# Stick-breaking attention with queries on partitions: weights from sigmoids and a backward product scan, in place of softplus sums on TensorE

## The chip, the cores and the metric

The kernel runs on one core of a Trainium2 chip. Its engines are TensorE (PE; its weight loads are listed apart as PEld), VectorE (DVE), ScalarE (ACT), GpSimd (POOL) and SyncE (SP). The metric is the device time of one execution in microseconds.

## The reference

Two transformer blocks are applied one after the other to x, 512 tokens of 1024 features, in float32. The change touches one stage of the second block, the stick-breaking attention with 16 heads of 64 features:

```
z = einsum("bhqd,bhkd->bhqk", q, k) / sqrt(64)
mask = key_pos < q_pos
log_beta = log_sigmoid(z)
log_1m = where(mask, log_sigmoid(-z), 0)
suffix = cumsum(log_1m, axis=keys, reverse=True) - log_1m
wts = where(mask, exp(log_beta + suffix), 0)
out = einsum("bhqk,bhkd->bhqd", wts, v)
```

The weight of key j for query i is thus sigmoid(z_ij) times the product of sigmoid(-z_il) over the keys l between j and i. The stage has a projection to q, k and v before it and an output projection with a residual after it.

## The kernel before

Activations lie with features on partitions and the 512 tokens along the free side, in eight tiles of 128 features. Products keep float32's precision by splitting each operand into two parts (hi and lo) of the type fp32r: ScalarE casts hi, VectorE subtracts to get lo, and a product is three passes (lo by hi, hi by lo, hi by hi; `mm3`, lines 171 to 176). One block of weights (128 output columns) is loaded by SyncE's queue (`raw`), split (`whi` on ScalarE, line 101; `wlo` on VectorE, line 102) and used in 24 products of 512 columns (`gemm`). `Feed` hands the blocks out in a fixed order, loaded three and split two blocks ahead, into buffers of a ring.

Heads are worked on in eight pairs k, since two heads of 64 features fill 128 partitions; half 0 and half 1 of a pair are the two heads. The scores of a head are held with keys on partitions: block j of 128 keys against the queries that can see it, 512, 384, 256 and 128 columns, in three PSUM banks (`ZG`: keys 0; keys 1 and 3; keys 2). Per half-step:

- `scores` (line 1108): twelve products from the parts of q and k (line 1117), then for each of three groups the softplus max(z, 0) + ln(1 + exp(-|z|)) in three ScalarE passes (1121 to 1123) and one VectorE pass (1124), a causal select on GpSimd (1094), and a split into parts `sp`.
- `sums` (line 1129): twenty products that add -softplus, summed over the later keys, onto the scores in PSUM, with a triangle or ones (`ntri`) as the other operand (1134).
- `weights` (line 1137): exp of the result, the causal select again, and a split into parts `w`.
- `values` (line 1147): twelve products with v (line 1154), and a split of the output (`Oh`, `Ol`).

TensorE's order in this stage is the order of the code (`manual_schedule`); the other engines' lists are ordered by the scheduler. Between the steps of a pair the code puts the projections for the next pairs (q and k by `proj`, v in two halves, then turned to tokens on partitions by four transposes in `vparts`), and for the last two pairs parts of the output projection (`out_part`).

Of the kernel before, what the change touches and what calls it, by code (L numbers as in the profile page):

```python
# [25 lines left out]
# columns of the packed per-feature vectors  # L26
# [9 lines left out]
# square constants  # L36
# [3 lines left out]
# order of the 128-column blocks of w_in  # L40
# [13 lines left out]
def block_kernel(ctx: ExitStack, tc: tile.TileContext, xT, pT, cols, cst, wA, wBr, wO, w13, w2, wPG, wPL,  # L54
# [107 lines left out]
    feed.add([bQKV[8], bQKV[9], bQKV[0], bQKV[10], bQKV[11]])  # L162
    for k in range(KD - 1):
        if k == KD - 2:
            feed.mark((2, 0, 0, 1))
        feed.add(([bQKV[9 + 2 * (k + 2)]] if k < KD - 2 else [bO[0]]) + [bQKV[k + 1]] + ([bQKV[8 + 2 * (k + 2)]] if k < KD - 2 else []))
    feed.add([bO[m] for m in range(1, KD)])
# [59 lines left out]
    def rowbc(pool, tag, c4, name):  # L227
        """[128, 4] per token -> psum [128, 512], the same on every partition."""
# [12 lines left out]
    def norm_rows(pool, tag, ss, name, rc=None):  # L241
        """1/rms of each token, spread over the partitions."""
# [15 lines left out]
    # =========================== block 1, mixers ===========================  # L258
# [30 lines left out]
    with ExitStack() as ca:  # L289
# [73 lines left out]
        # (the slots of the residual are free until the output projection)  # L363
# [29 lines left out]
        # g4: per token and head, [beta, alpha, i, f]  # L393
# [6 lines left out]
        # softplus(alpha), softplus(-f)  # L400
# [24 lines left out]
        # gl: [-exp(a_log) softplus | log f], negated: lg2[:, 0] = -g, lg2[:, 1] = -log f  # L425
# [9 lines left out]
        # cum[:, 0] inclusive cumsums within a block, cum[:, 1] block totals; [.., 0] g, [.., 1] log f  # L435
# [3 lines left out]
        bge = GP.tile([P, NB, H], F32, name="bge")    # beta exp(gc)  # L439
# [5 lines left out]
        kds = GP.tile([P, NB, H], F32, name="kds")    # exp(gtot - gc)  # L445
# [116 lines left out]
        # rj[:, j]: exponent row for the keys of block j  # L562
# [117 lines left out]
        def solve(i):  # L680
            """U = (I + beta K K^T * decay)^-T of chunk i, and what follows from it"""
# [67 lines left out]
        def state(i):  # L749
# [24 lines left out]
            # head norm  # L774
# [6 lines left out]
            # q carries rq / sqrt(dk)  # L781
# [127 lines left out]
    # =========================== per-layer embedding gate, then the recurrent mixer ===========================  # L909
    RP = ctx.enter_context(tc.tile_pool(name="RP", bufs=1, side="right", reuse_waits="tile"))  # L910
    B = xset(RP, "B")
    with ExitStack() as cb:
# [29 lines left out]
        # R1: block 1's final norm; R2: block 2's first norm of its result  # L942
# [24 lines left out]
        ls2 = PB.tile([P, KD], F32, name="ls2")      # -2 log sigmoid(lam)  # L967
# [7 lines left out]
        def branch(n):  # L975
            """input blocks 2n and 2n + 1, convolved, with their parts"""
# [17 lines left out]
        def recur(n, xc, xp_):  # L994
            hi, lo = parts_of(load_raw(aRI[n]), 8, PB, "rw")
            y, ti, v, a = b2("y"), b2("ti"), b2("v"), b2("a")
            for m in range(2):
# [4 lines left out]
                V.tensor_scalar(y[:, m, :], y[:, m, :], 1.0, ls2[:, k:k + 1], op0=ALU.add, op1=ALU.mult)   # -log_a / 2  # L1002
# [6 lines left out]
            # 1 - a = v (1 + a), sqrt(1 - a^2) = sqrt(v) (1 + a)  # L1009
# [5 lines left out]
            hs = b2("hs")                                # half of the state  # L1015
# [4 lines left out]
        def outgate(k, h_):  # L1020
            """h gelu(gate), gelu(x) = x / 2 (1 + tanh(c (x + 0.044715 x^3)))"""
# [20 lines left out]
        # the first block's result, normed  # L1042
# [29 lines left out]
    # =========================== stick-breaking attention ===========================  # L1072
    with ExitStack() as cs:
        pmm = cs.enter_context(tc.tile_pool(name="pmm3", bufs=2, space=PSUM, reuse_waits="tile"))
        psz = cs.enter_context(tc.tile_pool(name="psz", bufs=2, space=PSUM, reuse_waits="tile"))
# [5 lines left out]
        ntri = SB.tile([P, 2, P], F32R, name="ntri")  # L1081
        S.activation(ntri[:, 0, :], CST[:, C_TL, :], AF.Copy, scale=-1.0)
        S.activation(ntri[:, 1, :], ones, AF.Copy, scale=-1.0)
# [3 lines left out]
        # blocks of keys in three banks: 0 | 1, 3 | 2  # L1087
# [3 lines left out]
        def causal(t, js):  # L1091
            for j in js:
                o = ZP[j][1]
                G.affine_select(t[:, o:o + P], t[:, o:o + P], pattern=[[1, P]], base=0, channel_multiplier=-1,
                                compare_op=ALU.is_gt, fill=0.0)
# [8 lines left out]
        def blk(ts, j):  # L1104
            g, o = ZP[j]
            return ts[g][:, o:o + NW[j]]

        def scores(half, qp, kp):
            p0 = 64 * half
            zs = [psz.tile([P, T], F32, tag=f"z{g}", bufs=2, name=f"z{g}") for g in range(2)] + [zlast[:, half, :]]  # L1110
            sps = []
            for g, (w, js) in enumerate(ZG):
                z = zs[g]
                for j in js:
                    ks = slice(j * P, (j + 1) * P)
                    for n, (a, b) in enumerate(((kp[1], qp[0]), (kp[0], qp[1]), (kp[0], qp[0]))):
                        TE.matmul(blk(zs, j), a[p0:p0 + 64, ks], b[p0:p0 + 64, j * P:], start=(n == 0 and j == js[0]),  # L1117
                                  stop=False, skip_group_check=True)
                e = SB.tile([P, T], F32, tag="e", bufs=4, name="e")
                es = e[:, 0:w]  # L1120
                S.activation(es, z[:, 0:w], AF.Abs)
                S.activation(es, es, AF.Exp, scale=-1.0)
                S.activation(es, es, AF.Ln, bias=onec)
                V.scalar_tensor_tensor(es, z[:, 0:w], 0.0, es, op0=ALU.max, op1=ALU.add)
                causal(e, js)
                sps.append(parts(f"sp{g}", es, w, 1))
            return zs, sps
# [9 lines left out]
        def weights(zs):  # L1137
            out = [None] * 3
            for g in (2, 1, 0):
                w, js = ZG[g]  # L1140
                e = SB.tile([P, T], F32, tag="e", bufs=4, name="e2")
                S.activation(e[:, 0:w], zs[g][:, 0:w], AF.Exp)
                causal(e, js)
                out[g] = parts(f"w{g}", e[:, 0:w], w, 1)
            return out

        def values(k, half, wts, vp):
            po = pn.tile([P, T], F32, tag="nr", name="po")
            n = 0
            for g in (2, 1, 0):  # L1150
# [10 lines left out]
        with tc.issue_after(last.ins):  # L1161
            S.preload_act_table_set("natural_log_exp_and_others")
        def evac(ps, w):
# [241 lines left out]
```

## Time and profile before

| | |
|---|---|
| three timed runs | 2107.92, 2108.28 (median), 2108.46 us |
| span of the profiled execution, first to last instruction | 2105.6 us |
| busy: TensorE, VectorE, ScalarE, GpSimd | 2074.4, 1087.7, 825.9, 241.7 us |
| attention stage, first scores to the last pair's values | 1457.1 to 1704.7 us |

The profile gives no time for the profiled execution apart from its span, which lies 2.7 us under the median. Busy times are sums of durations; where operations overlap (TensorE's above all), the distance between starts says what one costs.

### The profile page before, as it was taken

The numbers are of one execution on the slowest core, as the hardware profiler recorded it, in microseconds if no ns is written. First come the engines' busy times: TensorE is split into PE (matmuls) and PEld (weight loads), VectorE is DVE, ScalarE is ACT, GpSimd is POOL, SyncE is SP. The second block draws the span as 40 slices with busy tenths as digits, with TensorE's granted clock in tenths as the row PEclk, the third lists the DMA queues.
The fourth block names the chain that finished last, engine by engine and source line by source line (L and its number), as shares of the span: only waits on it lengthen the run. The fifth ranks groups of instructions, "written<-read, shape, count | busy, mean of one in ns | idle before, by whom it ended". The sixth has DMA issues, their size and how long they took to land.

```text
span 2105.6 us, 24834 instructions
## 1 busy us (share of the span) xinstructions
PE 2074.4 (99%) x9946; PEld 1726.6 (82%) x9946; DVE 1087.7 (52%) x1461; ACT 825.9 (39%) x1213; POOL 241.7 (11%) x293
## 2 busy tenths in 40 slices
PE   8999999999999999999999999999999999999998
PEld 7778899888888888877788888887888888888887
DVE  5667454555444432779954444334666554444322
ACT  4333232333233222546633233224778743233221
POOL 0111000131000000252310000001212220000011
PEclk9999999999999999999999999999999999999999
DMA  4211111333322333322223323332111122323332
GB/s 166 70 61 60 51 50 41 107 123 100 100 92 99 95 99 97 110 80 82 87 93 99 100 92 97 94 99 90 42 59 61 40 71 90 100 92 98 93 100 68
DMA packets 53667, 181.73 MB, mean 86 GB/s; under 512 B 5808, under 2 KB 7984, under 8 KB 53552
## 3 DMA queue, kind: packets, MB, share of 16 engines
q1 hardware_dynamic: 53408, 180.05, 27.0%
q8 instruction: 78, 1.28, 0.3%
q14 instruction: 37, 0.30, 0.0%
q10 hardware_dynamic: 144, 0.10, 0.0%
HBM read 178.03 MB, written 2.10 MB: 86 GB/s over the span
## 4 chain that ended last, share of the span: by engine, by line
PE 92%; DVE 4%; issue 1%; DMA 1%; ACT 1%; POOL 0%; SPq 0%; POOLq 0%; DVEq 0%
PE psmm L174 19%; PE psmm L175 19%; PE psmm L176 19%; PE psd L174 5%; PE psd L175 5%; PE psd L176 5%; PE z L1134 2%; PE po L1154 1%; PE z L1117 1%; PE pU L732 1%; PE pX L727 1%; DVE wlo L102 1%; DVE xc L988 1%; PE psv L174 1%; PE psv L176 1%
## 5 line engine op out<-in xcount | busy, mean ns | idle before, releaser
L101 ACT CAST whi<-raw 128x1024 fp32r<-128x1024 f32 (+1 forms) x333 | 344.2, 1035 | 923.2 <-issue 363.5
L102 DVE TENSOR_TENSOR wlo<-raw,whi 128x1024 fp32r<-128x1024 f32 (+1 forms) x333 | 411.3, 1236 | 292.9 <-ACT whi L101 292.7
L174 PE MATMUL psmm<-Bh,wlo 128*128 128x512 f32 x1032 | 402.4, 390 | 0.0
L175 PE MATMUL psmm<-Bl,whi 128*128 128x512 f32 x1032 | 402.0, 390 | 0.1
L176 PE MATMUL psmm<-Bh,whi 128*128 128x512 f32 x1032 | 401.9, 389 | 0.0
L174 PE MATMUL psmm<-Ah,wlo 128*128 128x512 f32 x832 | 332.9, 401 | 4.0 <-DVE wlo L102 3.1
L176 PE MATMUL psmm<-Ah,whi 128*128 128x512 f32 x832 | 325.2, 391 | 0.0
L175 PE MATMUL psmm<-Al,whi 128*128 128x512 f32 x832 | 324.4, 390 | 0.6 <-DVE Al L190 0.6
L174 PEld LDWEIGHTS psmm<-Bh,wlo 128*128 128x128 f32 x1032 | 193.7, 188 | 41.2 <-DVE wlo L102 0.2
L175 PEld LDWEIGHTS psmm<-Bl,whi 128*128 128x128 f32 x1032 | 193.8, 188 | 40.4 <-DVE Bl L190 0.5
L176 PEld LDWEIGHTS psmm<-Bh,whi 128*128 128x128 f32 x1032 | 193.8, 188 | 39.9
L217 POOL TENSOR_TENSOR ss<-ss,sq 128x512 f32<-128x512 f32 x55 | 84.9, 1550 | 1133.3 <-issue 803.9
L174 PE MATMUL psd<-Hh,wlo 128*128 128x512 f32 x506 | 196.8, 389 | 0.0
L175 PE MATMUL psd<-Hl,whi 128*128 128x512 f32 x506 | 196.8, 389 | 0.0
L176 PE MATMUL psd<-Hh,whi 128*128 128x512 f32 x506 | 196.8, 389 | 0.0
L174 PEld LDWEIGHTS psmm<-Ah,wlo 128*128 128x128 f32 x832 | 156.4, 188 | 37.2 <-DVE wlo L102 4.5
L176 PEld LDWEIGHTS psmm<-Ah,whi 128*128 128x128 f32 x832 | 156.2, 188 | 33.7
L175 PEld LDWEIGHTS psmm<-Al,whi 128*128 128x128 f32 x832 | 156.6, 188 | 30.3 <-DVE Al L190 1.1
L871 DVE TENSOR_TENSOR u<-psmm,R 128x512 f32<-128x512 f32 x66 | 45.6, 691 | 194.2 <-PE psmm L176 194.2
L867 DVE TENSOR_TENSOR s<-psmm,R 128x512 f32<-128x512 f32 x66 | 45.6, 692 | 137.0 <-PE psmm L176 134.1
L176 PEld LDWEIGHTS psd<-Hh,whi 128*128 128x128 f32 x506 | 95.0, 188 | 19.9
L174 PEld LDWEIGHTS psd<-Hh,wlo 128*128 128x128 f32 x506 | 95.0, 188 | 19.7
(500 smaller groups left out, 2617.6 us busy)
## 6 DMA issues: line engine op xcount, KB each, us to landing
raw<-in_f SPq DMA_DIRECT2D x120, 512.0 KB, 3.5
raw<-in_w SPq DMA_DIRECT2D x60, 512.0 KB, 3.5
raw<-in_wA SPq DMA_DIRECT2D x43, 512.0 KB, 3.5
raw<-in_bQKV SPq DMA_DIRECT2D x24, 512.0 KB, 3.5
raw<-in_aIn SPq DMA_DIRECT2D x16, 512.0 KB, 3.6
raw<-in_f SPq DMA_DIRECT2D x16, 384.0 KB, 3.0
x<-in_xT SPq DMA_DIRECT2D x16, 256.0 KB, 3.4
raw<-in_wBr SPq DMA_DIRECT2D x8, 512.0 KB, 3.5
```

Source lines behind the costliest of these rows:

```text
L101: copied[0] = S.copy(hi[:, :nk, :], raw[:, :nk, :])
L102: V.tensor_tensor(lo[:, :nk, :], raw[:, :nk, :], hi[:, :nk, :].bitcast(F32), op=ALU.subtract)
L174: TE.matmul(ps, l, xh, start=(first and i == 0), stop=False)
L175: TE.matmul(ps, h, xl, start=False, stop=False)
L176: TE.matmul(ps, h, xh, start=False, stop=(last and i == n - 1))
L217: eng.tensor_tensor(self.acc, self.acc, sq, op=ALU.add)
L727: heads(lambda h: TE.matmul(pX[:, h], Nm[:, h, :], odd(U)[:, h], start=True, stop=True))
L732: heads(lambda h: TE.matmul(pU[:, h], Tt[:, h, :], X[:, h], start=True, stop=True))
L867: V.tensor_tensor(s1, p1, R, op=ALU.mult)
L871: V.tensor_tensor(u, p3, R, op=ALU.mult)
L988: V.scalar_tensor_tensor(ac, cx[:, j:j + T], col("aconv", 4 * k + j), ac, op0=ALU.mult, op1=ALU.add)
L1134: TE.matmul(blk(zs, j)[:, (jj - j) * P:], ntri[:, 0 if jj == j else 1, :], sp[:, o:o + NW[jj]], start=False, stop=(jj == j and sp is sps[g ...
```

## The change

Scores are now held with queries on partitions: query block i against the keys it can see, 128 (i + 1) columns, again in three PSUM banks (`QB`: queries 3; queries 2 and 0; queries 1), now one buffer each instead of two. 1/rms of the query's token and 1/8 become the per-partition scale `rq` of the activation, so q is split straight from PSUM, without the scaling by R. Per group, ScalarE writes `om` = sigmoid(-z) and `be` = sigmoid(z); GpSimd sets the masked part of `om` to 1 and of `be` to 0; VectorE runs a scan backward over the keys, pr = max(om * state, anew), where `anew` is 1 at the last column of each query block and 0 elsewhere, so that the product starts anew there; and `be` is multiplied by `pr` moved by one column. `turn` transposes the ten 128x128 blocks of weights on TensorE into three banks, in the old layout, and splits them. The softplus, the sums, and their split are gone. In the loop over pairs, the scores of the next head are issued ahead of the transposes of the one before; K of the next pair is now projected in the pair before it instead of two pairs ahead, and a fourth block of the output projection is begun early.

```diff
-        zlast = psz.tile([P, 2, 256], F32, tag="z2", bufs=1, name="zlast")
-        R = norm_rows(pn, "nr", ss, "R6")
+        psz = cs.enter_context(tc.tile_pool(name="psz", bufs=1, space=PSUM, reuse_waits="tile"))
+        rc6 = norm_cols(pn, "nr", ss)
+        R = norm_rows(pn, "nr", ss, "R6", rc6)
+        rq = SB.tile([P, 2, NB], F32, name="rq")
+        for n, c in enumerate((0.125, -0.125)):
+            V.tensor_scalar(rq[:, n], rc6, c, None, op0=ALU.mult)
+        QB = ((0, 3, 0, 512), (1, 2, 0, 384), (1, 0, 384, 128), (2, 1, 0, 256))
+        ZW = ((0, 512), (512, 512), (1024, 256))
         def scores(half, qp, kp):
+            for g in range(3):
+                qbs = [(i, o, w) for g_, i, o, w in QB if g_ == g]
+                for i, o, w in qbs:
+                    qs = slice(p0, p0 + 64), slice(i * P, (i + 1) * P)
+                    for n, (a, b) in enumerate(((0, 1), (1, 0), (0, 0))):
+                        TE.matmul(zs[g][:, o:o + w], qp[a][qs], kp[b][p0:p0 + 64, 0:w], start=(n == 0 and o == 0),
+                                  stop=(n == 2), skip_group_check=True)
+                c0, cw = ZW[g]
+                for t, n in ((om, 1), (be, 0)):
+                    for i, o, w in qbs:
+                        S.activation(t[:, c0 + o:c0 + o + w], zs[g][:, o:o + w], AF.Sigmoid, scale=rq[:, n, i:i + 1])
+                    d0 = c0 + qbs[0][1] + qbs[0][2] - P
+                    d = t[:, d0:c0 + cw].rearrange("p (n c) -> p n c", c=P)
+                    G.affine_select(d, d, pattern=[[0, len(qbs)], [-1, P]], base=0, channel_multiplier=1,
+                                    compare_op=ALU.is_gt, fill=float(n))
+                sl = slice(c0, c0 + cw)
+                V.tensor_tensor_scan(pr[:, sl][:, ::-1], om[:, sl][:, ::-1], anew[:, sl][:, ::-1], 1.0,
+                                     op0=ALU.mult, op1=ALU.max)
+                V.tensor_tensor(be[:, c0:c0 + cw - 1], be[:, c0:c0 + cw - 1], pr[:, c0 + 1:c0 + cw], op=ALU.mult)
+            return be
+        def turn(be):
+            out = []
             for g, (w, js) in enumerate(ZG):
+                t = pn.tile([P, T], F32, tag="nr", name="t2") if g == 2 else psz.tile([P, T], F32, tag=f"t{g}", name=f"t{g}")
                 for j in js:
+                    for i in range(j, NB):
+                        c = next(ZW[g_][0] + o for g_, i_, o, _ in QB if i_ == i) + j * P
+                        o = ZP[j][1] + (i - j) * P
+                        TE.transpose(t[:, o:o + P], be[:, c:c + P], ident)
+                out.append(parts(f"w{g}", t[:, 0:w], w, 1))
-        def sums(zs, sps):
-            for j in (3, 2, 1, 0):
-                for jj in range(3, j - 1, -1):
-                    g, o = ZP[jj]
-                    for sp in (sps[g][1], sps[g][0]):
-                        TE.matmul(blk(zs, j)[:, (jj - j) * P:], ntri[:, 0 if jj == j else 1, :], sp[:, o:o + NW[jj]],
-                                  start=False, stop=(jj == j and sp is sps[g][0]), skip_group_check=True)
             for k in range(KD):
+                more = k < KD - 1
+                wb = scores(1, q, kk)
+                wt = turn(wa)
                 if more:
+                    kk, q = proj(k + 1, 1), qn
+                    values(k, 0, wt, v)
                     vhi, vlo = feed.next(bQKV[k + 1])
                     pv = pmm.tile([P, T], F32, tag="mm", name="psv")
                     mm3(pv, [(vhi[:, c, :], vlo[:, c, :], A[c]) for c in range(4)], last=False)
+                    wa = scores(0, q, kk)
+                    wt = turn(wb)
                     mm3(pv, [(vhi[:, c, :], vlo[:, c, :], A[c]) for c in range(4, 8)], first=False)
                     vt = evac(pv, 2)
+                    if k < KD - 2:
+                        qn = proj(k + 2, 0)
+                    else:
+                        out_part(0, range(0, 6))
+                    values(k, 1, wt, v)
+                    v = vparts(vt)
                 else:
+                    out_part(1, range(0, 7))
+                    values(k, 0, wt, v, psz, "z0")
+                    out_part(0, range(6, 7))
+                    wt = turn(wb)
+                    out_part(2, range(0, 7), psz, "z1")
+                    values(k, 1, wt, v, psz, "z0")
+            out_part(3, range(0, 7), psz, "z2")
+            for m in range(4):
                 out_part(m, range(7, 8))
```

On TensorE, where one pair's V transposes (`pv`) are followed by the next half-step, the list before goes on with the twenty sums into the score banks (`z`, `zlast`; `sp` are the parts of softplus), and then the other head's scores from q and k:

```order
L1175 MATMUL pv<-CST,qk 128x128 x4
L1134 MATMUL z_11500<-sp1l,ntri 128x128
L1134 MATMUL z_11500<-sp1h,ntri 128x128
L1134 MATMUL zlast<-sp1l,ntri 128x128
...
L1134 MATMUL z_11499<-sp0l,ntri 128x512
L1134 MATMUL z_11499<-sp0h,ntri 128x512
L1117 MATMUL z_11661<-qh,kl 128x512
L1117 MATMUL z_11661<-ql,kh 128x512
```

In the changed kernel the same place has the second head's scores at once, then the first head's ten transposes (`t` from `be`), then the projection of the next K:

```order
L1182 MATMUL pv<-CST,qk 128x128 x4
L1119 MATMUL z_11468<-kl,qh 128x512
L1119 MATMUL z_11468<-kh,ql 128x512
...
L1119 MATMUL z_11470<-kh,qh 128x256
L1146 MATMUL t_11512<-CST,be 128x128 x4
L1146 MATMUL t_11521<-CST,be 128x128 x4
L1146 MATMUL t_11530<-CST,be 128x128 x2
L173 MATMUL psmm<-Bh_6291,wlo 128x512
```

The twenty sums have gone, and ten transposes stand behind the scores instead of ahead of them.

On VectorE, at the same half-step, the list before has the splits of the weights `w`, then the softplus passes of the other head (`e`) and their splits (`sp`):

```order
L1101 TENSOR_TENSOR vl<-pv,vh 128x512
L1101 TENSOR_TENSOR w2l<-e_11639,w2h 128x256
L1101 TENSOR_TENSOR w1l<-e_11646,w1h 128x512
L1101 TENSOR_TENSOR w0l<-e_11654,w0h 128x512
L1124 SCALAR_TENSOR_TENSOR e<-z_11661,e 128x512
L1124 SCALAR_TENSOR_TENSOR e<-z_11662,e 128x512
L1124 SCALAR_TENSOR_TENSOR e<-zlast,e 128x256
L1101 TENSOR_TENSOR sp0l<-e,sp0h 128x512
```

In the changed kernel the scans of the new scores (`pr` from `om`; this listing names a scan by the form that it is encoded in) and the products (`be`) come first, and the splits of the transposed weights of the head before (`w0l`, `w1l`, `w2l`) stand behind and between the last of them:

```order
L1104 TENSOR_TENSOR vl<-pv,vh 128x512
L1131 SCALAR_TENSOR_TENSOR pr<-om,anew 128x512
L1134 TENSOR_TENSOR be<-be,pr 128x511
L1131 SCALAR_TENSOR_TENSOR pr<-om,anew 128x512
L1134 TENSOR_TENSOR be<-be,pr 128x511
L1131 SCALAR_TENSOR_TENSOR pr<-om,anew 128x256
L1104 TENSOR_TENSOR w0l<-t_11512,w0h 128x512
L1134 TENSOR_TENSOR be<-be,pr 128x255
L1104 TENSOR_TENSOR w1l<-t_11521,w1h 128x512
```

The splits that `values` of one head reads have moved from ahead of the other head's passes to behind that head's scans.

## Rows read from the trace of the kernel before

**Rows 1.** The page, section 1: busy us, share, instructions.

```profile
span 2105.6 us, 24834 instructions
...
PE 2074.4 (99%) x9946; PEld 1726.6 (82%) x9946; DVE 1087.7 (52%) x1461; ACT 825.9 (39%) x1213; POOL 241.7 (11%) x293
```

**Rows 2.** Windows from scores to scores: a full period, the first, the last.

```profile
core 0: us, PE busy (x) PEld busy (x) DVE busy (x) ACT busy (x) POOL busy (x), PEclk, DMA share, GB/s
...
1547.79:1578.68 30.89, 30.89 (x165) 26.35 (x165) 19.09 (x30) 22.99 (x44) 6.19 (x17) 1.00 0.17 52
...
1457.14:1486.01 28.87, 26.68 (x141) 22.32 (x140) 17.35 (x27) 21.04 (x41) 4.93 (x15) 1.00 0.17 55
1668.04:1705.71 37.67, 36.66 (x192) 31.22 (x192) 16.37 (x27) 22.24 (x44) 6.53 (x18) 1.00 0.05 15
```

**Rows 3.** Timeline of PE (start us, us), the first product of each step.

```profile
1544.92 0.22 PE L1134 MATMUL z<-sp1l,ntri 128*128 128x128 f32 x1
...
1547.79 0.50 PE L1117 MATMUL z<-qh,kl 64*128 64x512 f32 x1
...
1549.90 0.50 PE L174 MATMUL psv<-Bh,wlo 128*128 128x512 f32 x1
...
1552.77 0.39 PE L174 MATMUL psmm<-Bh,wlo 128*128 128x512 f32 x1
...
1558.21 0.28 PE L1154 MATMUL po<-w2h,vl 128*128 128x256 f32 x1
...
1560.14 0.60 PE L1175 MATMUL pv<-CST,qk 128*128 128x128 f32 x4
...
1563.43 0.49 PE L1117 MATMUL z<-qh,kl 64*128 64x512 f32 x1
```

**Rows 4.** Transposes on PE: eight in a timeline, and line 1175's durations.

```profile
195.01 1.04 PE L635 MATMUL po<-CST,x 128*128 128x128 f32 x8
...
L1175 PE MATMUL pv<-CST,qk x32: 270/272/327, 1459.3 to 1677.3; 128*128 128x128 f32 x32
```

**Rows 5.** Waits of PE, 1455 to 1700 us (total, times, longest), and one later.

```profile
PE z L1134 <- DVE sp1l L1101: 1.9, 2, 1.4
PE zlast L1134 <- DVE sp2l L1101: 1.3, 2, 0.8
...
1709.46 0.50 PE L174 MATMUL psmm<-Oh,wlo 128*128 128x512 f32 x1 [0.75 <-DVE wlo L102]
```

**Rows 6.** ACT on PSUM: timeline after scores, and two lines' min/median/max ns.

```profile
1548.90 0.60 ACT L1121 ACTIVATE e<-z 128x512 f32<-128x512 f32 x1
...
L1121 ACT ACTIVATE e<-z x32: 587/604/617, 1458.3 to 1683.9; 128x512 f32<-128x512 f32 x32
...
L1001 ACT ACTIVATE y<-pr,hb x8: 672/676/688, 940.5 to 1021.4; 128x512 f32<-128x512 f32 x8
```

**Rows 7.** DVE: a scan's min/median/max, and groups of 1455 to 1700 us.

```profile
L1017 DVE TENSOR_TENSOR_SCAN hs<-a,v x8: 1192/1213/2253, 963.2 to 1038.6; 128x512 f32<-128x512 f32 x8
...
L102 DVE TENSOR_TENSOR wlo<-raw,whi 128x1024 fp32r<-128x1024 f32 x22 | 26.9, 1221 | 6.1 <-ACT whi L101 6.1
L1124 DVE SCALAR_TENSOR_TENSOR e<-z,e 128x512 f32<-128x512 f32 x32 | 21.5, 687 | 16.5 <-ACT e L1123 16.5
...
L1101 DVE TENSOR_TENSOR w0l<-e,w0h 128x512 fp32r<-128x512 f32 x16 | 11.1, 692 | 4.7 <-ACT w0h L1100 4.7
...
L1101 DVE TENSOR_TENSOR sp2l<-e,sp2h 128x256 fp32r<-128x256 f32 x16 | 6.7, 418 | 0.0
```

**Rows 8.** Selects on POOL, and one beside a split on DVE.

```profile
L1094 POOL TENSOR_SCALAR_AFFINE_SELECT e<-e x128: 287/293/1272, 1463.1 to 1697.8; 128x128 f32<-128x128 f32 x128
...
L696 POOL TENSOR_SCALAR_AFFINE_SELECT tm<-tm x4: 632/636/642, 196.6 to 283.6; 128x512 f32<-128x512 f32 x4
...
1554.99 1.15 POOL L1094 TENSOR_SCALAR_AFFINE_SELECT e<-e 128x128 f32<-128x128 f32 x1 [0.30 <-DVE e L1124]
...
1554.78 1.22 DVE L102 TENSOR_TENSOR wlo<-raw,whi 128x1024 fp32r<-128x1024 f32 x1
```

More of the change, by code (lines that the diff above doesn't have):

```diff
@@ L161, in block_kernel @@
     ffn_plan(f13[0], f2[0])
-    feed.add([bQKV[8], bQKV[9], bQKV[0], bQKV[10], bQKV[11]])
+    feed.add([bQKV[8], bQKV[9], bQKV[0], bQKV[10]])
     for k in range(KD - 1):
[L164 to L167, printed above, removed]
+        feed.add([bQKV[9 + 2 * (k + 1)], bQKV[k + 1]] + ([bQKV[8 + 2 * (k + 2)]] if k < KD - 2 else []))
+    feed.mark((2, 0, 0, 1))
+    feed.add([bO[m] for m in range(KD)])
     feed.mark((0, 0, 1))
@@ L1074, in block_kernel @@
         pmm = cs.enter_context(tc.tile_pool(name="pmm3", bufs=2, space=PSUM, reuse_waits="tile"))
[L1075 to L1078 removed]
+        psz = cs.enter_context(tc.tile_pool(name="psz", bufs=1, space=PSUM, reuse_waits="tile"))
+        rc6 = norm_cols(pn, "nr", ss)
+        R = norm_rows(pn, "nr", ss, "R6", rc6)
         WP[2] = cs.enter_context(tc.tile_pool(name="wh5", bufs=1, side="right", reuse_waits="tile"))
         SB = cs.enter_context(tc.tile_pool(name="SB", bufs=1, reuse_waits="tile"))
[L1081 to L1083 removed]
+        rq = SB.tile([P, 2, NB], F32, name="rq")
+        for n, c in enumerate((0.125, -0.125)):
+            V.tensor_scalar(rq[:, n], rc6, c, None, op0=ALU.mult)
         O = xset(SB, "O")
         NW = (512, 384, 256, 128)
+        QB = ((0, 3, 0, 512), (1, 2, 0, 384), (1, 0, 384, 128), (2, 1, 0, 256))
+        ZW = ((0, 512), (512, 512), (1024, 256))
         ZG = ((512, (0,)), (512, (1, 3)), (256, (2,)))
         ZP = {0: (0, 0), 1: (1, 0), 3: (1, 384), 2: (2, 0)}
[L1091 to L1095, printed above, removed]
+        anew = SB.tile([P, 1280], F32, name="anew")
+        G.memset(anew, 0.0)
+        for g, _, o, w in QB:
+            c = ZW[g][0] + o + w - 1
+            G.memset(anew[:, c:c + 1], 1.0)
         def parts(name, src, w, bufs):
@@ L1102, in parts @@
             return hi, lo
-        def blk(ts, j):
-            g, o = ZP[j]
-            return ts[g][:, o:o + NW[j]]
         def scores(half, qp, kp):
             p0 = 64 * half
-            zs = [psz.tile([P, T], F32, tag=f"z{g}", bufs=2, name=f"z{g}") for g in range(2)] + [zlast[:, half, :]]
-            sps = []
+            zs = [psz.tile([P, T], F32, tag=f"z{g}", name=f"z{g}") for g in range(3)]
+            be = SB.tile([P, 1280], F32, tag="be", bufs=2, name="be")
+            om = SB.tile([P, 1280], F32, tag="om", bufs=2, name="om")
@@ L1137, in weights @@
[L1137 to L1144, printed above, removed]
-            return out
-        def values(k, half, wts, vp):
-            po = pn.tile([P, T], F32, tag="nr", name="po")
+                    for i in range(j, NB):
+                        c = next(ZW[g_][0] + o for g_, i_, o, _ in QB if i_ == i) + j * P
+                        o = ZP[j][1] + (i - j) * P
+                        TE.transpose(t[:, o:o + P], be[:, c:c + P], ident)
@@ L1149, in values @@
+                out.append(parts(f"w{g}", t[:, 0:w], w, 1))
+            return out
+        def values(k, half, wts, vp, pool=pmm, tag="mm"):
+            po = pool.tile([P, T], F32, tag=tag, name="po")
             n = 0
-            for g in (2, 1, 0):
+            for g in range(3):
                 for j in ZG[g][1]:
@@ L1176, in vparts, with out_part @@
             return [x.rearrange("p (b d) -> p b d", b=NB) for x in parts("v", pv.rearrange("p b d -> p (b d)"), T, 2)]
+        part = {}
+        def out_part(m, ks, pool=pmm, tag="mm"):
+            if m not in part:
+                part[m] = feed.next(bO[m]) + (pool.tile([P, T], F32, tag=tag, name="pso"),)
+            hi, lo, ps = part[m]
+            mm3(ps, [(hi[:, c, :], lo[:, c, :], O[c]) for c in ks], first=ks[0] == 0, last=ks[-1] == KD - 1)
         with tc.manual_schedule(engines={mybir.EngineType.PE}):
-            q, kk = proj(0, 0, psz, "z0"), proj(0, 1, psz, "z1")
+            q, kk = proj(0, 0), proj(0, 1)
             vt = proj(0, 2)
+            wa = scores(0, q, kk)
             qn = proj(1, 0)
-            z0, s0 = scores(0, q, kk)
             v = vparts(vt)
-            kn = proj(1, 1)
-            part = {}
-            def out_part(m, ks, pool=pmm, tag="mm"):
-                if m not in part:
-                    part[m] = feed.next(bO[m]) + (pool.tile([P, T], F32, tag=tag, name="pso"),)
-                hi, lo, ps = part[m]
-                mm3(ps, [(hi[:, c, :], lo[:, c, :], O[c]) for c in ks], first=ks[0] == 0, last=ks[-1] == KD - 1)
-            for k in range(KD):
-                more, more2 = k < KD - 1, k < KD - 2
-                sums(z0, s0)
-                w0 = weights(z0)
-                z1, s1 = scores(1, q, kk)
-                kk, q = kn, qn
-                if more2:
-                    kn = proj(k + 2, 1)
-                elif more:
-                    out_part(0, range(0, 3))
-                else:
-                    out_part(1, range(0, 7))
-                values(k, 0, w0, v)
+            for k in range(KD):
+                more = k < KD - 1
+                wb = scores(1, q, kk)
+                wt = turn(wa)
                 if more:
+                    kk, q = proj(k + 1, 1), qn
+                    values(k, 0, wt, v)
                     vhi, vlo = feed.next(bQKV[k + 1])
@@ L1210, in block_kernel @@
                     mm3(pv, [(vhi[:, c, :], vlo[:, c, :], A[c]) for c in range(4)], last=False)
-                else:
-                    out_part(0, range(6, 7))
-                    out_part(2, range(0, 4), psz, "z0")
-                sums(z1, s1)
-                w1 = weights(z1)
-                if more:
-                    z0, s0 = scores(0, q, kk)
+                    wa = scores(0, q, kk)
+                    wt = turn(wb)
                     mm3(pv, [(vhi[:, c, :], vlo[:, c, :], A[c]) for c in range(4, 8)], first=False)
                     vt = evac(pv, 2)
-                if more2:
-                    qn = proj(k + 2, 0)
-                elif more:
-                    out_part(0, range(3, 6))
-                else:
-                    out_part(2, range(4, 7))
-                values(k, 1, w1, v)
-                if more:
-                    v = vparts(vt)
-            for m in range(3):
+                    if k < KD - 2:
[4 more added lines that the diff above has]
+                    v = vparts(vt)
+                else:
+                    out_part(1, range(0, 7))
[6 more added lines that the diff above has]
+            for m in range(4):
                 out_part(m, range(7, 8))
@@ L1232, in block_kernel @@
         for m in range(KD):
[L1233 removed]
+            ps = part[m][2] if m in part else gemm(psz, bO[m], O, tag=("z0", "t0", "t1", "z1")[m % 4])
             V.tensor_tensor(x_tiles[m], ps, x_tiles[m], op=ALU.add)
```

28 lines of the change are left out of this document (8 added, 20 removed).

## The prediction

> **What bounds the kernel now.** I read the page's busy table first: TensorE is busy 2074.4 of 2105.6 us [rows 1], so whatever leaves TensorE's own list shortens the program, and whatever is added elsewhere costs only when TensorE has to wait for it. Busy shares can hide such waits, so next I cut the attention stage into windows, each from the first score product of one pair of heads to that of the next [rows 2]. In a full period of 30.89 us TensorE is busy all of it at granted clock 1.00 (the 2.4 GHz level), VectorE 19.09, ScalarE 22.99, GpSimd 6.19 us. Only the first pair's window (26.68 of 28.87) and the last one (36.66 of 37.67) have idle time on TensorE. So the stage is TensorE's list of products, and VectorE has 11.8 us a period to spare.
>
> The timeline of TensorE gives that list's prices as distances between starts, which is what counts where products overlap [rows 3]. From first start to next first start: the sums over keys 1547.79 - 1544.92 = 2.87 us; a set of scores 1549.90 - 1547.79 = 2.11; half of a V projection 1552.77 - 1549.90 = 2.87; a whole projection (24 products) 1558.21 - 1552.77 = 5.44, or 0.227 each; a set of values 1560.14 - 1558.21 = 1.93. The four transposes of V and one set of sums together are 1563.43 - 1560.14 = 3.29, which leaves 0.42 for the transposes.
>
> **What is removed from TensorE.** The sums: 20 products in each of 16 half-steps (8 pairs, 2 heads), 16 x 2.87 = 45.9 us. The scores keep their twelve products of the same four widths (only the stationary and the moving side change places), values keep theirs, the projections are the same 24 + 8 blocks. These I cost at no change.
>
> **What is added to TensorE.** Ten 128x128 transposes per half-step. A set of eight transposes takes 1.04 us from first start to last end and one lasts 0.272 [rows 4], so the starts are (1.04 - 0.27)/7 = 0.11 apart. The V transposes say 0.42/4 = 0.105. Ten are 1.1 us; 16 x 1.1 = 17.6. The gain is 45.9 - 17.6 = 28.3 us. From below the price is 0.105 each (gain 29.1); from above, if a transpose cost its whole 0.272, 2.72 a set (gain 2.4). I take 0.11, since eight in a row are the nearest to four, four and two in a row.
>
> The Trainium skill has a sentence that speaks against this change: "TensorE: Matmul & The Clock Gate", Part 4, gives about 275 ns for a transpose in one kernel's context and says that the output then still has to be copied out of PSUM. The duration agrees with the 272 ns row; taken as the cost of each in a row, it makes ten of them 2.75 us and the trade almost even. The trace's starts 0.11 apart say that these durations overlap.
>
> **Waits that go.** In the first and the last pair the sums wait for the split of softplus: 1.9 and 1.3 us in total [rows 5]. With no sums there is nothing that waits so: in the new order the first transposes stand behind a projection, the V transposes and the second scores, 2.11 + 5.44 + 0.42 + 2.11 = 10.1 us after the first score product, and the weights are ready at 9.1 (next part). I count -3.2.
>
> **The wait that may come.** New weights pass two sigmoids per row group (ScalarE), a causal select on each (GpSimd), a scan and a product (VectorE); and the transposed blocks are then split on ScalarE and VectorE as before. VectorE takes its list in order, and there the split of the *previous* half's transposed blocks stands behind the *new* half's scans: w0l after all three scans, then a product, w1l, w2l. So `values` of the first head in each pair waits for the second head's scans. Prices: the first activation starts 1548.90 - 1547.79 = 1.1 after the scores start and a PSUM activation of 512 takes 0.604 to 0.676 [rows 6] (the table function with a per-partition operand is nearest: 0.68; no sigmoid is in the trace); a scan of 512 1.21 (1.19 to 2.25), so 0.66 for 256 (an estimate: half of the columns, plus a fixed part of about 0.1), a product or split of two operands 0.69 for 512 and 0.42 for 256, a weight split 1.22 [rows 7]. No scan in the trace runs over reversed operands; its bounds are those two ends. A select of 128 columns takes 0.29, of 512 0.64 [rows 8]; the new 256-wide one lies between, 0.40.
>
> One more row decides how these add up. A select that began at 1554.99, when VectorE had just started a 1.22 us weight split at 1554.78, lasted 1.15 instead of 0.29, up to the end of that split [rows 8]. So a select and a VectorE operation on two SBUF operands took turns. Scans and products have two SBUF operands each, so I put them and the selects one after another. From the first score product: om 1.8; its select and handover 2.2; scan 3.4; select be 3.7; select om of group 1 4.1; product 4.8; scan 6.0; select 6.4; product 7.1; select 7.4; scan 8.0; w0l 8.7; product 9.1; w1l 9.8; w2l 10.2.
>
> TensorE comes to these values at 2.11 + 1.1 + 5.44 = 8.65; counted by columns out of the 1.93 us, w0l is needed 0.3 later (8.95, no wait) and w1l 0.95 later (9.6): a wait of 0.2, with the handover between engines **0.4 us**. Queued behind are the V projection's half and the second scores, so the whole wait shows in the time. In the second half another 2.87 of V projection lies in between, 11.5 against 10.2: no wait. Seven pairs give 2.8 us. The last pair has 21 products in place of 24 there (4.8 us): values at 8.0, waits for w0l, w1l and w2l, about 1.0. Without the taking of turns, w1l is ready 1.4 earlier and all these are zero; that is the lower bound. The Trainium skill, "SBUF — State Buffer", Who interferes with whom, states this as a rule: a VectorE instruction with two SBUF inputs and a GpSimd one that reads SBUF exclude each other for the whole instruction. By the rule the sum has the 3.8 us, without it none; the 1.15 us row agrees.
>
> **Edits at nothing.** VectorE per half-step loses three max-add passes and three splits (2 x 0.687 + 0.42 and 2 x 0.69 + 0.42, 3.6 us) and gains 2 x 1.21 + 0.66 + 2 x 0.69 + 0.42 = 4.9; per period 19.09 + 2 x 1.3 - 0.69 (Q is no longer scaled there) = 21.0 of about 27.8. It is hidden as long as it stays under the period, with 3.4 us per half-step to spare, though the list's order makes the 0.4 above. ScalarE loses four passes per group for two and stays under its 22.99. The score banks are single now: both heads share z0 to z2, but between their uses lie 8 us or more and the sigmoids end 4.3 after the scores start. At the end the weights of block 4 need a buffer that block 0 frees, as one did before (TensorE's 0.75 us wait for a weight split [rows 5]); three more products on either side of it, so I leave it.
>
> **Sum.** 2105.6 - 28.3 - 3.2 + 2.8 + 1.0 = 2077.9 us of span. The page gives no time for its execution apart from the span; the timed runs' median of 2108.28 lies 2.7 above it, so **2080.6 us**. One period should be 30.89 - 2 x 1.77 + 0.4 = 27.75.
>
> **Rivals.**
> (a) *Taking turns is worse than I laid out*: scans near their longer rows, or selects that wait for weight splits too. Each further 0.1 us per half-step costs about 1.5 us. For it: VectorE's list leaves `w2l` and then the K projection's scaling only just ahead of TensorE (the scaling ends at 10.9, and the values end at 8.65 + 1.93 + 0.4 = 11.0). Against: 6.8 us of VectorE per period are free. With 0.3 to 1.5 us per half-step: 2085 to 2104 us.
> (b) *The scan is the bound, and the kernel slower.* If scans run at 2.25 (reversed operands, or GpSimd holding each one), a half-step has 2 x 1.04 + 0.55 = 2.6 us more. The first halves pass all of it on (8 x 2.6), the second ones all but about 0.5 (7 x 2.1): +35.5, 2116 us. Break-even lies at +2.1 us per half-step, three scans of 5.2 us instead of 3.1. For it: the 2.25 us row; against: the median of those eight scans is 1.21, so most ran unhindered.
> (c) *A transpose costs its duration*: gain 2.4 instead of 28.3, 2080.6 + 25.9 = 2106.5, no change. Against: rows 4.
>
> **Chances.** My forecast (waits up to 0.3 us per half-step away from those counted) 0.60: 2074 to 2085. (a) 0.24. (b) 0.12, a quarter of it near no change. (c) 0.04. The low end takes 0.105 us transposes and no new wait: 2105.6 - 29.1 - 3.2 + 2.7 = 2076.0, with 2 us for the tail's waits: 2074. The high end reaches into (a) at about 1.1 us per half-step: 2098; above it lie some 0.17. Differences under 0.2% (4.2 us) can't be told from none: (a), with my forecast, is faster; (c) and a quarter of (b) same; the rest of (b) slower. Faster 0.84, same 0.07, slower 0.09.
>
> **What would show it.** Right: a period of 27.5 to 28 us in the windows; transposes with starts 0.11 apart; the only repeated TensorE wait at `po`, for w0l or w1l, below 0.6 us; no wait in the second halves. Wrong: scans of 2 us or more, VectorE above 25 us a period, waits of TensorE at the transposes (weights late) or at `psv` (scaling of K late).

## The result and the profile after

The changed kernel takes **2082.12 us** (median of 4 runs, 2080.03 to 2083.57), the kernel before 2108.37 beside it (2107.92 to 2111.86): ratio 0.9863, 95% interval 0.9846 to 0.988. The forecast was 2080.6, faster. The profiled execution's span is 2080.2 instead of 2105.6 us.

The page's first section, to be read beside [rows 1]: TensorE has 160 instructions less (320 products for sums gone, 160 transposes new) and 22.5 us less to do, and it is still busy 99% of the span.

```profile
span 2080.2 us, 24373 instructions
...
PE 2051.9 (99%) x9786; PEld 1705.2 (82%) x9786; DVE 1104.5 (53%) x1455; ACT 763.9 (37%) x1099; POOL 257.1 (12%) x266
```

Windows of the changed kernel, to be read beside [rows 2]: the first is a full period, from the first score product of one pair of heads to that of the next; the others are 2 us each at the change from the seventh pair to the last.

```profile
core 0: us, PE busy (x) PEld busy (x) DVE busy (x) ACT busy (x) POOL busy (x), PEclk, DMA share, GB/s
1514.23:1541.66 27.43, 27.43 (x145) 23.26 (x144) 21.41 (x29) 15.31 (x31) 7.84 (x12) 1.00 0.20 59
1652.00:1654.00 2.00, 1.44 (x7) 1.12 (x8) 0.63 (x2) 0.59 (x1) 0.00 (x0) 0.88 0.25 98
1654.00:1656.00 2.00, 2.00 (x9) 1.90 (x8) 0.88 (x2) 1.27 (x2) 0.36 (x2) 0.50 0.00 0
1656.00:1658.00 2.00, 2.00 (x9) 1.78 (x10) 1.88 (x3) 1.97 (x6) 1.69 (x3) 0.50 0.00 0
1658.00:1660.00 2.00, 2.00 (x8) 1.81 (x8) 1.90 (x2) 1.57 (x4) 1.59 (x3) 0.50 0.00 0
1660.00:1662.00 2.00, 2.00 (x9) 1.59 (x9) 2.00 (x5) 0.00 (x0) 0.00 (x0) 0.91 0.00 0
```

Two things are to be seen. A full period is 27.43 us with TensorE busy all of it: the wait forecast in each pair is absent. And near the end the granted clock stands at 0.50 (1.2 GHz) for three windows; in the kernel before it is 1.00 in all three windows of [rows 2], the last pair's among them. The waits of TensorE between 1430 and 1780 us (in total, times, longest) say what came just ahead:

```profile
PE pv L1182 <- DVE Ol L1162: 1.4, 1, 1.4
PE psmm L173 <- DVE wlo L102: 0.6, 1, 0.6
PE psmm L173 <- DVE Ol L1162: 0.3, 1, 0.3
```

The four waits for parts of softplus [rows 5] are gone, the tail's wait for `wlo` is nearly as before, and a wait of 1.40 us at the V transposes is new. TensorE's timeline (start us, us) shows a regular half-step, and from 1650.88 on this wait:

```profile
1514.23 0.50 PE L1119 MATMUL z<-kl,qh 64*128 64x512 f32 x1
...
1516.36 1.31 PE L1146 MATMUL t<-CST,be 128*128 128x128 f32 x10
1517.42 0.48 PE L173 MATMUL psmm<-Bh,wlo 128*128 128x512 f32 x1
...
1523.01 0.39 PE L1157 MATMUL po<-w0h,vl 128*128 128x512 f32 x1
1523.24 0.39 PE L1157 MATMUL po<-w0l,vh 128*128 128x512 f32 x1
...
1523.87 0.35 PE L1157 MATMUL po<-w1l,vh 128*128 128x384 f32 x1
...
1650.88 0.28 PE L1157 MATMUL po<-w2h,vh 128*128 128x256 f32 x1
1652.57 0.66 PE L1182 MATMUL pv<-CST,qk 128*128 128x128 f32 x4 [1.40 <-DVE Ol L1162]
1653.15 0.50 PE L1119 MATMUL z<-kl,qh 64*128 64x512 f32 x1
...
1656.67 2.39 PE L1146 MATMUL t<-CST,be 128*128 128x128 f32 x10
1658.72 0.77 PE L173 MATMUL pso<-Oh,wlo 128*128 128x512 f32 x1
...
1660.14 0.49 PE L173 MATMUL pso<-Oh,wlo 128*128 128x512 f32 x1
```

In the regular half-step a set of scores takes 1516.36 - 1514.23 = 2.13 us and ten transposes 1517.42 - 1516.36 = 1.06, so 0.106 each. Behind the wait, scores take 1656.67 - 1653.15 = 3.52 us, transposes 2.05, and three output products 1.42 instead of 0.70. That is 1.4 + 1.0 + 0.7 = 3.1 us on top of the 1.40.

The reason for the wait stands in the order of the program. `pmm`, the pool of PSUM tiles for projections and values, has two banks. In the seventh pair `out_part(0)` holds one from 1644.91 on, so the V transposes need the bank of the values just ahead of them, which VectorE must empty first (`Ol`).

VectorE's and GpSimd's timeline of the same half-step shows the chain that I had laid out by hand:

```profile
1516.38 1.22 DVE L1131 TENSOR_TENSOR_SCAN pr<-om,anew 128x512 f32<-128x512 f32 x1 [0.15 <-POOL om L1128]
1517.73 0.88 DVE L1134 TENSOR_TENSOR be<-be,pr 128x511 f32<-128x511 f32 x1
1518.53 1.42 DVE L1131 TENSOR_TENSOR_SCAN pr<-om,anew 128x512 f32<-128x512 f32 x1
1520.06 0.78 DVE L1134 TENSOR_TENSOR be<-be,pr 128x511 f32<-128x511 f32 x1
1520.76 0.68 DVE L1131 TENSOR_TENSOR_SCAN pr<-om,anew 128x256 f32<-128x256 f32 x1
1521.36 0.66 DVE L1104 TENSOR_TENSOR w0l<-t,w0h 128x512 fp32r<-128x512 f32 x1
...
1522.27 0.68 DVE L1104 TENSOR_TENSOR w1l<-t,w1h 128x512 fp32r<-128x512 f32 x1
1522.87 0.41 DVE L1104 TENSOR_TENSOR w2l<-t,w2h 128x256 fp32r<-128x256 f32 x1
...
1516.06 0.29 POOL L1128 TENSOR_SCALAR_AFFINE_SELECT om<-om 128x128 f32<-128x128 f32 x1 [9.68 <-PE z L1119]
1516.64 1.06 POOL L1128 TENSOR_SCALAR_AFFINE_SELECT be<-be 128x128 f32<-128x128 f32 x1 [0.28 <-ACT be L1124]
1517.66 0.40 POOL L1128 TENSOR_SCALAR_AFFINE_SELECT om<-om 128x256 f32<-128x256 f32 x1
...
1518.83 1.21 POOL L1128 TENSOR_SCALAR_AFFINE_SELECT om<-om 128x128 f32<-128x128 f32 x1
```

`w0l` is done at 1522.02 and read at 1523.24; `w1l` is done at 1522.95 and read at 1523.87. So they are 1.2 and 0.9 us early, where I had them late.

### The profile page after: what moved, and what is told of

The parts are those of the page before. It is cut to its first block, busy times and chain, and to the rows that moved or that the text cites. A ratio compares the mean times of both kernels' runs of the same rounds, so it can differ in the third digit from the quotient of the medians.

```text
span 2080.2 us, 24373 instructions
## 1 busy us (share of the span) xinstructions
PE 2051.9 (99%) x9786; PEld 1705.2 (82%) x9786; DVE 1104.5 (53%) x1455; ACT 763.9 (37%) x1099; POOL 257.1 (12%) x266
## 4 chain that ended last, share of the span: by engine, by line
PE 91%; DVE 5%; ACT 1%; issue 1%; POOL 1%; DMA 1%; SPq 0%; POOLq 0%; DVEq 0%; ACTq 0%
PE psmm L173 19%; PE psmm L174 19%; PE psmm L175 19%; PE psd L173 6%; PE psd L175 6%; PE psd L174 6%; PE z L1119 2%; PE po L1157 1%; DVE wlo L102 1%; PE pU L731 1%; PE pX L726 1%; PE t L1146 1%; DVE xc L987 1%; PE psv L173 1%; PE psv L174 1%
## 5 line engine op out<-in xcount | busy, mean ns | idle before, releaser
L174 PEld LDWEIGHTS psd<-Hl,whi 128*128 128x128 f32 x506 | 95.0, 188 | 19.8
```

What stands on the lines that cost most here:

```text
L174: TE.matmul(ps, h, xl, start=False, stop=False)
```

## Experiments

The kernel before took 2110.18 us beside the first four runs, 2109.42 beside the next four and 2110.18 beside the last three. Half-steps are distances between the first transposes of neighbouring sets; in full periods of the changed kernel they alternate between 13.52 and 13.91 us.

**e1_po_bank: the new wait, taken away.** The seventh pair's second values go into a bank of `psz`, so the V transposes find a free one.

```
-                    values(k, 1, wt, v)
+                    if k < KD - 2:
+                        values(k, 1, wt, v)
+                    else:
+                        values(k, 1, wt, v, psz, "z2")
```

> The changed kernel, but the values of the seventh pair's second head go into score bank z2 instead of the projections' two banks. In the changed kernel TensorE waits 1.40 us there (V transposes wait for Ol), and right behind that wait the granted clock falls to 0.5 for 7 us, which stretches the scores from 2.12 to 3.52 us and the transposes from 1.06 to 2.05. Theory: the wait is the cause of the lower clock, so both go: no wait at pv, clock 1.00 throughout, span 4.5 us shorter (about 2075.7, time 2077.6). Rival: the clock falls for another reason at that place (the mix of narrow products and transposes): only the wait goes, 1.4 us, and the windows still show a stretch at 0.5.

Measured 2078.7 us, ratio 0.9853 (0.9838 to 0.9868), span 2076.3. The granted clock stays at 1.00 through the stage, here in the 10 us around the same V transposes, and of TensorE's waits one is left:

```profile
1650.00:1660.00 10.00, 10.00 (x58) 8.60 (x57) 7.16 (x11) 5.86 (x13) 3.92 (x6) 1.00 0.19 54
...
PE psmm L173 <- DVE wlo L102: 0.6, 1, 0.6
```

The span is 3.9 us shorter than the changed kernel's, against 1.40 + 3.1 = 4.5 worked out above. From the first set of transposes to the last the difference is 4.9 us (200.64 instead of 205.55), with the wait of 0.3 us gone too; the other 1.0 us went the other way ahead of these sets and behind them, where the two programs are the same.

**e2_rq_align: another size of the first small tile.** O and the tiles behind it move by 96 bytes per partition. The reason for asking: products that read O start 0.70 us apart per three, against 0.68 before.

```
-        rq = SB.tile([P, 2, NB], F32, name="rq")
+        rq = SB.tile([P, 2, 4 * NB], F32, name="rq")
```

> The changed kernel, but the small tile rq, which stands ahead of O in its pool, is 128 bytes a partition instead of 32. In the changed kernel the output projection's products start 0.233 us apart, in the one before 0.227. Theory: O's place in memory (shifted by 32 bytes) makes its reads slower; with 128 bytes they start 0.227 apart again, 64 x 3 products x 0.0065 = 1.3 us. Rival: the spacing has to do with something else (neighbours in the new order); no change in spacing or time.

Measured 2082.11 us, ratio 0.9868 (0.9853 to 0.9883), span 2077.8. The spacing stayed at 0.70, so this padding did nothing to it. What I had not expected: the same wait of 1.40 us at the V transposes is in this trace, and the granted clock is 1.00 behind it, in windows of 2 us from the V transposes on:

```profile
1653.00:1655.00 2.00, 1.69 (x9) 1.39 (x10) 0.63 (x2) 0.64 (x2) 0.00 (x0) 1.00 0.18 72
1655.00:1657.00 2.00, 2.00 (x18) 1.86 (x17) 1.28 (x2) 2.00 (x5) 1.01 (x2) 1.00 0.00 0
1657.00:1659.00 2.00, 2.00 (x11) 1.66 (x10) 1.88 (x3) 2.00 (x6) 1.97 (x4) 1.00 0.00 0
```

So the wait and the fall of the clock are two things.

**e3_transposes_twice.** Each transpose of `turn` is done twice, into the same place.

> The changed kernel with each of the ten transposes of a half-step issued twice into the same place (the output stays the reference's). Theory: a transpose in a row costs the distance of the starts, 0.11 us: ten more are 1.1 us a half-step, the period grows by 2.2 us, the time by 16 x 1.1 = 18 us, to about 2100, less where the added time covers a wait. Rival: each costs its duration of 0.273 us: 2.7 us a half-step, 44 us in all, to about 2126.

Measured 2098.3 us, ratio 0.9944 (0.9929 to 0.9959). Half-steps are 14.58 and 15.04 us, so ten more transposes cost 1.06 to 1.13, and the run 16.2 us more than the changed kernel's time (17.6 by spans). A transpose in a row costs 0.10 to 0.11 us of TensorE.

**e4_scans_twice.** Each scan is done twice with the same result, 2 x 1.22 + 0.68 = 3.1 us more of VectorE per half-step.

> The changed kernel with each scan issued twice (the output stays the reference's): VectorE has 3.3 us more per half-step, what the prediction's second rival would cost it. Theory (its list in order, values waiting for w0l, w1l): the first halves have a margin of 0.9 us in the changed kernel, the second ones about 2; so waits of 2.4 and 1.3 us, 8 x 2.4 + 7 x 1.3 = 28 us, time about 2110, with TensorE's waits at po for w0l or w1l, and the granted clock may fall behind them. Rival: VectorE's free time (6.0 of 27.4 us a period) takes nearly all of it, 0 to 5 us.

Measured 2108.98 us, ratio 0.999 (0.998 to 0.9999), span 2106.9: all of the gain is gone. TensorE's waits in the stage show the mechanism of rival (b), the weights late and then the scaled keys (until these are scaled, their bank of `pmm` is not free):

```profile
PE psv L173 <- DVE qk L1173: 8.1, 6, 2.1
PE po L1158 <- DVE qk L1173: 4.9, 7, 1.8
PE po L1158 <- DVE w0l L1104: 4.3, 7, 1.9
```

The expected time of about 2110 came out, but not by the expected sum: full periods are 14.69 + 15.58 = 30.27 us, 2.8 more than the changed kernel's 27.43 where 2.4 + 1.3 = 3.7 was expected, and still below the 30.89 of the kernel before. The first, the sixth and the seventh pair lose more, and the granted clock fell to 0.50 twice, behind a wait of 1.95 us in the first pair and one of 1.40 at the V transposes of the seventh.

**e9_third_scan_twice: how much room the chain has.** e1 with only the scan over 256 columns done twice, +0.68 us per half-step.

> e1 with the scan over 256 columns (0.68 us) done twice, the second with the same result, so that VectorE's chain ends 0.68 us later in each half-step. Theory (from the trace of the changed kernel: the weight splits are ready 0.9 to 1.2 us before values needs them): no repeated new wait of TensorE, within 1 us of e1, near 2079. Rival (the chain is as laid out in the prediction, with a wait of 0.4 us in each pair already): +0.68 us in 8 half-steps, +5.4 us, near 2084.

Measured 2079.81 us, ratio 0.9857 (0.9841 to 0.9874), span 2078.7. Half-steps in full periods stay at 13.52 and 13.91; of the 2.4 us of span over e1, 1.9 arise in the first pair (+0.45) and in the sixth and seventh (+0.6 and +0.9). A chain with a wait already in each pair would have passed 0.68 on eight times. So the regular chain has at least 0.68 us of room.

**e7_sums_back: the removed TensorE time alone, put back** into the changed kernel ahead of the transposes (`t` is overwritten by these).

```
+                if g == 0:
+                    for w_ in (128, 128, 256, 128, 256, 384, 128, 256, 384, 512):
+                        for _ in range(2):
+                            TE.matmul(t[:, 0:w_], A[1][0][:, 0:P], A[0][0][:, 0:w_], start=True, stop=True)
```

> The changed kernel with the removed TensorE time put back by itself: 20 products of the same ten widths as the sums over keys, each twice, ahead of the transposes of every half-step, with operands that are there already; their result is overwritten. Theory (the gain is the sums' own time, 2.87 us a half-step): 16 x 2.87 = +45.9, near 2128 us, since the chain on VectorE then has more cover and no new wait. Rival (part of the removed 45.9 was a wait of the sums, or the new chain costs that much): clearly below +45.9 us, say +35.

Measured 2124.82 us, ratio 1.0072 (1.0057 to 1.0087), span 2121.3. TensorE's timeline gives the price of the 20 products, 1497.94 - 1495.07 = 2.87 us, as in [rows 3]:

```profile
1495.07 3.03 PE L1145 MATMUL t<-Bh,Bh 128*128 128x128 f32 x20
1497.94 1.25 PE L1150 MATMUL t<-CST,be 128*128 128x128 f32 x10
1511.40 3.03 PE L1145 MATMUL t<-Bh,Bh 128*128 128x128 f32 x20
```

Half-steps became 16.33 and 16.75, +2.82 each. The whole run rose by 42.7 us (41.1 by spans) and not by 45.9. Two pieces make up most of the difference: the changed kernel's clock fall (3.1 us) is not in this trace, though its wait of 1.40 us is, and the half-steps of 13.75 and 14.70 us in the sixth and seventh pair, where the changed kernel has small waits, are 16.33 here like the others, which saves 1.4. Beside the kernel before, the span is 15.7 us longer (2121.3 - 2105.6); the ten transposes of each half-step (17.6), less the four waits gone (3.2), with the new wait (1.4) and O's place (1.2, below) would be 17.0. So the new order of the list costs nothing large besides.

**e6_gap_midstage: does a wait of this kind lower the clock?** e1 (with e2's padding) and one more tile in the fourth pair, which takes a bank of `pmm` away until VectorE has read it.

```
+                        if k == 3:
+                            gap = pmm.tile([P, T], F32, tag="mm", name="gap")
+                            TE.transpose(gap[:, 0:P], vt[:, 0:P], ident)
+                            gs = SB.tile([P, 16], F32, name="gs")
+                            held = gap
...
+                    if k == 3:
+                        V.tensor_copy(gs, held[:, 0:16])
```

> The last full pair's second values write into a score bank, as in e1, so that its wait of TensorE at the V transposes (1.4 us) is gone; instead one extra tile in the middle of the stage (pair 3) takes a values bank away, so that there the same wait of about 1.4 us arises in a full period. Question: is it the wait itself that brings TensorE's clock down to 0.50 behind it? Theory 'any such gap does it': 1.4 + 0.1 (the extra transpose) + about 3.1 us over e1, near 2083.3 us of time, with the granted clock near 0.50 in the 7 us behind the gap. Rival 'the gap alone does not, it depends on where it falls and varies between executions': +1.5 us, near 2080.2, granted clock 1.00 behind it.

Measured 2079.79 us, ratio 0.9859 (0.9844 to 0.9874), span 2079.2. The wait is 1.0 us, and the granted clock falls to 0.50 behind it, here in the middle of the stage; the next half-step is 14.84 instead of 13.5 us:

```profile
1574.00:1575.00 1.00, 1.00 (x6) 1.00 (x6) 1.00 (x1) 1.00 (x4) 0.93 (x1) 0.50 0.00 0
```

The time over e1's (1.1 us) lies near the rival's +1.5, the profiled execution's span (2.9 us over e1's) contains the fall. One wait in one trace can't tell how often it happens, so:

**e11_four_gaps: the same wait in pairs 2 to 5**, on top of e8 (below).

> e8 with the extra tile of e6 in pairs 1 to 4, so that TensorE waits about 1.0 us at the V transposes in four full periods, with the same work around each wait. Theory (such a gap can lower the clock, but not each one does): 4 x (1.0 + 0.1) = +4.4 us for the waits and transposes, and 1.8 to 3.1 us more behind each gap with a clock of 0.50, where it appears; between 2080.8 (clock 1.00 behind all) and 2093 (lowered behind all). Rival (the gap does nothing to the clock, e6's fall had another cause): +4.4 us, 2080.8, and a granted clock of 1.00 behind all four.

Measured 2084.23 us, ratio 0.9873 (0.9856 to 0.9889), span 2081.3. TensorE waits 0.96 us at each of the four. Windows of 2 us, each beginning 2.0 to 3.0 us behind the end of one of these waits:

```profile
1518.00:1520.00 2.00, 2.00 (x11) 2.00 (x11) 1.88 (x3) 2.00 (x7) 1.97 (x3) 0.50 0.01 4
1548.00:1550.00 2.00, 2.00 (x15) 1.83 (x15) 1.81 (x2) 2.00 (x7) 1.69 (x4) 1.00 0.07 27
1576.00:1578.00 2.00, 2.00 (x18) 1.86 (x17) 1.23 (x1) 2.00 (x6) 1.32 (x3) 1.00 0.39 160
1605.00:1607.00 2.00, 2.00 (x17) 1.78 (x16) 1.50 (x2) 2.00 (x6) 1.67 (x3) 1.00 0.18 70
```

One fell, three did not. The half-steps with a wait are 15.17 to 15.19 instead of 13.89, +1.3 each; the one behind the fall is 15.13 instead of 13.48, +1.65, the others 13.48 to 13.49. By these 4 x 1.3 + 1.65 = 6.9 us over e8, against 7.4 by times and 5.9 by spans of e10_e8_again. "Can, but need not" stands; the rival falls.

**e8_o_offset, and both versions on one chip.** e1 with the first tile padded to 1024 bytes per partition, as large as the triangles of the kernel before:

```
-        rq = SB.tile([P, 2, NB], F32, name="rq")
+        rq = SB.tile([P, 2, 32 * NB], F32, name="rq")
```

> e1 with the small tile of scale factors padded to 1024 bytes per partition, so that the attention output O lies behind a first tile as large as the triangles were in the kernel before. Theory (the place of O makes the output projection's products start 0.233 us apart instead of 0.227): spacing back to 0.227, 192 products x 0.006 = -1.2 us against e1, near 2077.5 us. Rival (it is not the place): spacing 0.233, no difference to e1, near 2078.7.

> The same program as e1 again, beside e10_e8_again on one chip: near 0.9853 of the kernel before, output products 0.233 us apart.

> The same program as e8 again, on the chip of e10_e1_again. Theory (the place of O costs 0.006 us in each of its 192 products): 1.2 us less than e10_e1_again, with spacing 0.227. Rival (e8's 2 us were a difference between chips): no difference.

e8 measured 2076.42 us, ratio 0.9842 (0.9827 to 0.9857). On one chip e1's program took 2078.34 us (2077.73 to 2079.31) and e8's 2076.84 (2076.28 to 2077.81): 1.5 us less, with 1.2 expected, and spans of 2076.3 and 2075.4. The durations (min/median/max) and first and last starts of 32 output products, e1's program and then e8's:

```profile
L173 PE MATMUL psmm<-Oh,wlo x32: 393/396/468, 1679.5 to 1701.3; 128*128 128x512 f32 x32
```

```profile
L173 PE MATMUL psmm<-Oh,wlo x32: 389/389/470, 1678.8 to 1700.0; 128*128 128x512 f32 x32
```

The same stretch of 96 products takes 21.8 us in the one and 21.2 in the other; the other 96 output products stand ahead of it in pieces, and with the same spacing they make it 1.2 us. So where O and the tiles behind it lie in SBUF is worth between 0.9 us (by spans) and 1.5 us (by times). Why, no run shows. e8 is the fastest version that I found.

## Why the prediction was right, and where not

*The gain is the sums' own time on TensorE less that of the transposes*: right. 2.87 came back as 2.87 in e7, and 0.11 per transpose as 0.106 in the trace and 0.10 to 0.11 in e3. A half-step got 1.73 us shorter ((30.89 - 27.43) / 2), 16 x 1.73 = 27.7 against 28.3; scores at 2.13 for 2.11, and products spaced 0.23 just behind the transposes, are part of the difference. Rival (c), the transpose at its duration, falls: by its 0.272 e3 would have cost 44 us, and it cost 16 to 18.

*The waits that go* (-3.2): right, all four are gone.

*The wait that may come* (0.4 us per pair, 1.0 in the last): **this term was mis-sized, it measured 0 in the full periods.** The mechanism was there: a select that met a scan lasted 1.06 and 1.21 us instead of 0.29, until the scan's end; scans and products next to selects took 1.42 and 0.88 instead of 1.22 and 0.69. The Trainium skill ("SBUF — State Buffer", Who interferes with whom) says that a VectorE instruction with two SBUF inputs contends with a GpSimd one that reads SBUF, and calls it an exclusive lock. The trace agrees that a select is held until the scan's end, but not that whole durations add up: the product at 1517.73 ran beside a select of 0.40 us (1517.66) and took 0.19 more. What I got wrong is the price of taking turns: I added each whole select behind the scan, but the held ones ended 0.1 us behind the scan's end (1517.70 and 1520.04 against 1517.60 and 1519.95). [rows 8] had shown as much: that select ended at 1556.14, the split at 1556.00. And VectorE's records overlap by up to 0.1 us (the third scan starts at 1520.76, the product ahead of it ends at 1520.84). From the first scan's start to the end of `w1l` the chain took 6.6 us, where I had 7.6 (2.2 to 9.8). e9 confirms the room in full periods. Only in the sixth and seventh pair are there small waits (one half-step each of 13.75 and 14.70 us): in the seventh the scans start 4.3 us behind the first score product instead of 2.15, behind a weight split that comes later there, and the values wait 0.3 us for `w0l` and 0.2 for `w1l`.

*Break-even of rival (b)* at +2.1 us per half-step: also too early by that 1.0. e4, at +3.1, comes out at 0.999 of the kernel before, two falls of the clock included. No scan over reversed operands took 2 us (1.22 to 1.43 for 512 columns); (b) did not occur, nor did (a).

*The tail I left alone*: the wait for `wlo` is 0.6 for 0.75, as said. But **the step "so I leave it" overlooked the new 1.40 us wait**: I went through the score banks for new conflicts and not through the two of `pmm`, in which `out_part(0)` now sits across the V transposes. With the clock's fall behind it, it cost 1.4 + 3.1 = 4.5 us, of which e1's span gave back 3.9. O's place cost another 1.2.

By spans, 2080.2 against 2077.9, the result thus holds misses of opposite sign: no wait in the pairs (-3.8), then at the end the new wait, the clock and O's place (1.4 + 3.1 + 1.2), 0.6 in the half-steps, and 1.4 in those two of the sixth and seventh pair: +3.9, where +2.3 was measured. Of the other 1.6, 0.5 lies ahead of the stage (first scores at 1451.17 instead of 1457.14, 6.0 us earlier, where one projection of 5.44 went behind them); 1.1 has no name. So the gain was forecast by its mechanism, but that the time came within 2 us is partly luck: the misses nearly cancel.

## What to carry to other kernels

Where one engine is busy all of a period, cost a change by distances between starts on that engine, not by durations: that gave 28.3 us for sums against transposes, and the half-steps show 27.7. Lay out a chain on two engines that hold each other with the *remainder* of a held instruction, not with all of it. When a list of products is reordered, go through each pool of banks and ask who holds one across the new order: the one new wait that counted was there.

## What was not expected of the hardware

Behind a TensorE wait of 0.96 us or more, with work of the same kind on either side, the granted clock fell to 0.50 in some cases and stayed at 1.00 in others: it fell behind the 1.40 us wait of the changed kernel and of e3 and not behind the same one in e2 and e7, behind the first of e11's four equal waits and not behind the other three. In e4 a wait of 2.15 us passed without a fall. No trace of the stage shows a fall without such a wait ahead of it: e1, e8 and e9, whose longest TensorE wait is 0.7 us, have none. A fall cost 1.5 to 3.1 us on top of the wait (e6, 1.3 of it in the next half-step; the changed kernel). What decides is open.

The place of the output tile in SBUF changed the spacing of the products that read it, 0.233 or 0.227 us, by 992 bytes per partition of padding; 96 bytes changed nothing. This too is left open.
